# Encoder layer with implicit long filters: the last sums of the spectra, Newton's steps and the direction sums in the filter stage placed on other engines

## The chip, the cores and the metric

The kernel runs on one core of a Trainium2 chip. The metric is the device time of one launch in microseconds. The engines are named as in the profile: PE is TensorE (matmuls), DVE is VectorE, ACT is ScalarE, POOL is GpSimd and SP is SyncE, which only starts transfers here. Each engine works through its own queue in order.

## The reference

The layer normalises its input `x` (1 x 1024 x 1024, f32), projects it, sends the projections through an S5 branch and a Hyena branch, merges both and adds the result to `x`. The change touches the input norm and the stage that makes the Hyena filters. What they compute:

```python
def rmsnorm(x, w):
    y = xf * lax.rsqrt(jnp.mean(xf * xf, axis=-1, keepdims=True) + RMS_EPS)
    return (y * w.astype(jnp.float32)).astype(x.dtype)

def hyena_filters(L, w1, b1, freq, w2, b2, w3, decay):
    ...
    h = jnp.sin(fr * (h @ w2.astype(f32) + b2.astype(f32)))
    h = h @ w3.astype(f32)
    h = h * (jnp.exp(-t * jnp.abs(decay.astype(f32))) + HY_SHIFT)
    h = h.reshape(L, HY_ORDER, HY_DIRS, HY_WIDTH)
    h_fwd, h_bwd = h[:, :, 0], h[:, :, 1]
    k = jnp.concatenate([h_fwd, jnp.zeros_like(h_fwd[:1]), jnp.flip(h_bwd[1:], axis=0)], axis=0)
    k = k * lax.rsqrt(jnp.sum(k * k, axis=0, keepdims=True) + HY_EPS)
    return jnp.fft.rfft(k, axis=0)
```

There are 1024 time steps, two orders and 1024 channels, so 2048 filters of length 2048, and for each its real spectrum.

## The kernel before

The filters are made in eight **units**: two orders `o` times four groups `cq` of 256 channels. The loop in `filters` runs `u` from 0 to 8 and writes three things into each other, a step of each at a time: `filter_time` of unit `u` (eight time blocks of 128 steps, in the order 4, 5, 6, 7, 0, 1, 2, 3), `filter_freq` of unit `u - 1` (twelve steps), and every third step one of `norm_in`, the input norm, which goes on through several units. `filter_norm` of unit `u - 1` is written at the start of a unit with a higher priority. From this text a scheduler makes the order of each engine's queue, and it puts in the waits between engines. A pool's `bufs` says how many buffers a name has; a write into one waits until its last reader is done.

`filter_time`, one block: two matmuls into PSUM give `g`; ScalarE makes the exponential `e`; VectorE multiplies, `e` = (`e` + 0.05) * `g` (L338); ScalarE squares it as `sq` (L342) and GpSimd adds the squares up in `acc` (L357). Then the *direction sums*: the sum and the difference of the two directions (L349, L350), on VectorE for the block numbers in `f_dve0` (first unit) or `f_dve` (the other seven), on GpSimd for the rest. For the first four blocks they go to `so` (one buffer), which is split into a high and a low half, `sh` on ScalarE (L109; VectorE in the first unit) and `sl` on VectorE (L113); for the last four they are `ss` and `sd`, used as they are.

`filter_norm` sums `acc` over the partitions with matmuls into `q`, takes the reciprocal root of two columns (`rsqrt`, L114 to L126), and corrects one row of `ss` of block 0. `norm_in` calls the same `rsqrt` once, with eight columns, and with the result scales the rows `xr` of the input on ScalarE. `rsqrt` starts from an integer guess and makes three Newton steps, each column by itself.

`filter_freq` turns the halves into spectra by matmuls. For `j` = 0 and 1 it makes two odd parts `po` (PSUM, two buffers, L404) and two even parts `pe` (L414); `eo` (ScalarE, L421) is a copy of one even part, `ke` (VectorE, one buffer) the two sums of the even parts. Out of `ke` and each `po` come the sum and the difference, `ko`, which has two buffers (L429, L430), and SP writes `ko` to `kspec` in DRAM (L431). So a unit makes four `ko` tiles of 128 x 1024.

Elsewhere, in `prefetch`, the weights are split by the form that the change brings to `ko`: `wlo` = -`whi` on ScalarE (L511), and a DMA that GpSimd starts adds `wraw` to it in place (L512).

After the last unit come the projections and the S5 branch, whose parameters are loaded through ScalarE's queue.

Of the kernel before, what the change touches and what calls it, by code (L numbers as in the profile page):

```python
# [12 lines left out]
ALU = mybir.AluOpType  # L13
AF = mybir.ActivationFunctionType
# [5 lines left out]
NCH = 256  # L20
# [80 lines left out]
class Trunk:  # L101
# [13 lines left out]
    def rsqrt(self, pool, out, v, n):  # L115

        V = self.nc.vector
        h = pool.tile([128, n], F, name="rsq_h", tag="rsq_h")
        V.tensor_scalar(out=out.bitcast(I32), in0=v.bitcast(I32), scalar1=-0.5, scalar2=float(0x5F3759DF),
                        op0=ALU.mult, op1=ALU.add)  # L120
        V.tensor_scalar(out=v, in0=v, scalar1=-0.5, scalar2=None, op0=ALU.mult)
        for _ in range(3):
            for c in range(n):
                y, z = out[:, c:c + 1], h[:, c:c + 1]
                V.scalar_tensor_tensor(out=z, in0=y, scalar=v[:, c:c + 1], in1=y, op0=ALU.mult, op1=ALU.mult)
                V.scalar_tensor_tensor(out=y, in0=z, scalar=1.5, in1=y, op0=ALU.add, op1=ALU.mult)  # L126

    def reduce_2pi(self, out, x, k):
        nc = self.nc
# [113 lines left out]
    def filters(self, ctx, top):  # L243
        tc = self.tc
        c2 = ExitStack()
        mk = lambda c, n, b, **kw: c.enter_context(tc.tile_pool(name=n, bufs=b, **kw))
        self.f_dve0, self.f_dve = (0, 1, 2, 3, 4, 5), (0, 3)
        sd = [None, mk(ctx, "f_sd1", 1)]
        self.f_w = mk(ctx, "f_work", 2)
        sd[0] = mk(c2, "f_sd0", 1, side="right")  # L250
# [137 lines left out]
    def filter_freq(self, o, cq, sds):  # L388

        nc = self.nc  # L390
# [18 lines left out]
        def even(b0, tiles):  # L409
            pe = pk.tile([128, 2, NCH], F, name="pe", bufs=2)  # L410
            n = len(tiles)
            for part in (1, 0):
                for i, t in enumerate(tiles):
                    nc.tensor.matmul(out=pe[:, part], lhsT=fe[:, b0 + 2 * part + t % 2], rhs=sd[t][part],  # L414
                                     start=part == 1 and i == 0, stop=part == 0 and i == n - 1)
            return pe

        def join(j, po):
            pe = even(8 * j + 4, (2, 3))
            eo = wp.tile([128, 2, NCH], F, name="eo", bufs=1)  # L420
            nc.scalar.copy(out=eo, in_=pe)  # L421
            yield
            pe = even(8 * j, (0, 1))
            ke = wp.tile([128, 2, 2, NCH], F, name="ke", bufs=1)
            nc.vector.tensor_tensor(out=ke[:, 0], in0=pe, in1=eo, op=ALU.add)
            nc.vector.tensor_tensor(out=ke[:, 1], in0=pe, in1=eo, op=ALU.subtract)
            for jj in (j, j + 2):
                ko = wp.tile([128, 4, NCH], F, name="ko")
                nc.vector.tensor_tensor(out=ko[:, 0:2], in0=ke[:, jj // 2], in1=po[jj], op=ALU.add)  # L429
                nc.vector.tensor_tensor(out=ko[:, 2:4], in0=ke[:, jj // 2], in1=po[jj], op=ALU.subtract)  # L430
                nc.sync.dma_start(out=self.kspec[o, cq, jj], in_=ko.rearrange("p a c -> p (a c)"))  # L431

        for j in range(2):
            po = {}
            for jj in (j, j + 2):
                for po[jj] in odd(jj):
                    yield
            yield from join(j, po)
            yield
# [1043 lines left out]
```

## Time and profile before

| | |
|---|---|
| Median of 3 runs | 1446.65 us (1445.04 to 1446.68) |
| The profiled execution, whole | 1447.77 us |
| Its span | 1445.9 us |
| PE busy in the span | 1343.9 us, 93% |
| DVE | 1009.2 us, 70% |
| ACT | 515.7 us, 36% |
| POOL | 379.6 us, 26% |

The shares are means over stages that differ, and the change is made in one of them, the filters, which stand at the start (until about 260 us). So what counts is read there: a *window* is a stretch of the span, given in us from its start, with the busy time of each engine in it; a *wait* is idle time of an engine, put down to the instruction that ended it. "PEclk" is the clock that TensorE was granted, as a share of full speed, which is 2.4 GHz; the lower of the two levels is 1.2 GHz.

### The profile page before, as it was taken

How to read it: one execution, taken by the hardware profiler on the slowest of the kernel's cores; microseconds unless marked ns; L12 is line 12 of the kernel's file. 1: busy time of each engine (PE TensorE's matmuls, PEld its weight loads, DVE VectorE, ACT ScalarE, POOL GpSimd, SP SyncE). 2: the span in 40 equal slices, each digit the busy share in tenths (PEclk: the TensorE clock that was granted, in tenths of full speed). 3: DMA queues.
4: the chain of work that ended last, by engine and by line, in shares of the span. 5: the costliest groups of instructions: out<-in, count | busy, mean ns of one | idle time of the engine just before them, and what ended most of it. 6: DMA issues, size and time to landing. Idle time of an engine off the chain costs nothing.

```text
span 1445.9 us, 19569 instructions
## 1 busy us (share of the span) xinstructions
PE 1343.9 (93%) x7219; PEld 1132.4 (78%) x7219; DVE 1009.2 (70%) x1954; ACT 515.7 (36%) x737; POOL 379.6 (26%) x315
## 2 busy tenths in 40 slices
PE   5888999999999999999999999999999925999998
PEld 3776898888888887878788888888888825978886
DVE  7999997698689877224399994554379984842632
ACT  5576663223233332442322322533322213422322
POOL 3766774000000000232112100343311111432222
PEclk9998999999999999999999999999999967999999
DMA  8211225855784654667956569767788889666332
GB/s 277 90 73 73 89 110 144 199 154 140 201 264 109 139 127 84 167 159 223 315 162 172 178 175 282 195 175 200 254 265 267 268 253 306 184 175 160 119 115 73
DMA packets 188618, 257.23 MB, mean 178 GB/s; under 512 B 23069, under 2 KB 144153, under 8 KB 185788
## 3 DMA queue, kind: packets, MB, share of 16 engines
q1 hardware_dynamic: 149212, 153.69, 34.2%
q0 software_dynamic: 11520, 39.85, 14.6%
q10 hardware_dynamic: 27792, 62.45, 12.1%
q8 instruction: 57, 0.93, 0.3%
q14 instruction: 37, 0.30, 0.1%
HBM read 147.49 MB, written 76.82 MB: 155 GB/s over the span
## 4 chain that ended last, share of the span: by engine, by line
PE 66%; DVE 14%; DMA 8%; issue 2%; ACTq 0%; ACT 0%; SPq 0%; DVEq 0%
PE pps L541 42%; PE iv L634 6%; PE ops L1384 6%; DMA d_y<-x 3%; PE po L404 2%; DMA zc<-c_zc_lo_d 2%; PE fwo L685 2%; PE pe L414 1%; PE fwe L685 1%; DVE st L1216 1%; PE zt L670 1%; DVE st L1214 1%; PE s5ps L1166 1%; DVE e L338 1%; DVE m L719 1%
## 5 line engine op out<-in xcount | busy, mean ns | idle before, releaser
L512 POOL DMA_DIRECT2D wlo<-wraw x76 | 66.8, 879 | 717.8 <-ACT wlo L511 568.3
L541 PE MATMUL pps<-xh,whi 128*128 128x512 f32 x896 | 229.1, 400 | 3.2 <-DVE cv L565 3.2
L541 PE MATMUL pps<-xl,whi 128*128 128x512 f32 x896 | 224.3, 397 | 0.0
L541 PE MATMUL pps<-xh,wlo 128*128 128x512 f32 x896 | 223.9, 396 | 0.0
L541 PEld LDWEIGHTS pps<-xh,whi 128*128 128x128 f32 x896 | 165.9, 189 | 40.1 <-ACT wlo L511 3.6
L541 PEld LDWEIGHTS pps<-xh,wlo 128*128 128x128 f32 x896 | 166.5, 188 | 38.3
L541 PEld LDWEIGHTS pps<-xl,whi 128*128 128x128 f32 x896 | 166.2, 188 | 38.2 <-issue 0.2
L510 ACT CAST whi<-wraw 128x1024 fp32r<-128x1024 f32 (+1 forms) x76 | 74.7, 983 | 310.3 <-PE pps L541 267.9
L404 PE MATMUL po<-sh,fo 128*128 128x256 f32 x512 | 99.8, 289 | 6.9 <-DVE sh L111 5.7
L634 PEld LDWEIGHTS iv<-ic,y 128*128 128x128 f32 x752 | 96.3, 193 | 3.3 <-DVE y L113 0.6
L634 PE MATMUL iv<-ic,y 128*128 128x256 f32 (+1 forms) x752 | 97.7, 285 | 0.0
L113 DVE TENSOR_TENSOR y<-yraw,y 128x512 fp32r<-128x512 f32 x64 | 52.8, 837 | 55.4 <-ACT y L109 54.9
L404 PEld LDWEIGHTS po<-sh,fo 128*128 128x128 f32 x512 | 82.8, 194 | 9.8 <-DVE sh L111 6.7
L511 ACT ACTIVATE wlo<-whi 128x1024 fp32r<-128x1024 f32 (+1 forms) x76 | 74.9, 985 | 20.6 <-PE pps L541 20.4
L357 POOL TENSOR_TENSOR acc<-acc,sq 128x512 f32<-128x512 f32 x56 | 76.4, 1365 | 21.7 <-ACT sq L342 20.0
L404 PE MATMUL po<-sl,fo 128*128 128x256 f32 x256 | 73.4, 287 | 1.0 <-DVE sl L113 1.0
L109 ACT CAST y<-yraw 128x512 fp32r<-128x512 f32 x64 | 39.2, 620 | 76.2 <-PE iv L634 45.9
L563 DVE SCALAR_TENSOR_TENSOR cv<-pps,cw,cv 128x1023 f32<-128x1023 f32 x24 | 30.7, 1280 | 30.4 <-ACT cv L562 30.4
L685 PE MATMUL fwo<-z,zc 128*128 128x256 f32 x384 | 51.7, 288 | 0.0
L404 PEld LDWEIGHTS po<-sl,fo 128*128 128x128 f32 x256 | 49.5, 193 | 2.3 <-DVE sl L113 1.6
L685 PEld LDWEIGHTS fwo<-z,zc 128*128 128x128 f32 x384 | 50.1, 197 | 1.0
L333 PE MATMUL g<-w3h,ha 128*128 128x512 f32 x64 | 32.6, 510 | 18.4 <-DVE e L338 16.6
(437 smaller groups left out, 2662.4 us busy)
## 6 DMA issues: line engine op xcount, KB each, us to landing
wlo<-wraw POOLq DMA_DIRECT2D x64, 512.0 KB, 5.8
wraw<-w_in SPq DMA_DIRECT2D x56, 512.0 KB, 4.7
kspec<-ko SPq DMA_DIRECT2D x32, 512.0 KB, 3.0
kt<-kspec SPq DMA_DIRECT2D x32, 512.0 KB, 5.4
d_y<-x ACTq DMA_DIRECT2D x32, 512.0 KB, 3.9
yraw<-d_y SPq DMA_DIRECT2D x64, 256.0 KB, 4.9
d_m<-cv ACTq DMA_DIRECT2D x16, 512.0 KB, 2.7
d_z<-z ACTq DMA_DIRECT2D x8, 1024.0 KB, 6.1
```

The costliest lines, as they stand in the source:

```text
L109: nc.scalar.copy(out=hi, in_=src)
L113: e.tensor_tensor(out=lo, in0=src, in1=hi, op=ALU.subtract)
L333: nc.tensor.matmul(out=ps, lhsT=ha[:, tsl], rhs=w3h, start=True, stop=False)
L357: nc.gpsimd.tensor_tensor(out=acc, in0=acc, in1=sq, op=ALU.add)
L404: nc.tensor.matmul(out=po[:, part], lhsT=fo[a][:, 12 * (jj % 2) + b], rhs=sd[4 + i][d][:, part], start=n == 0 and part == 0, stop=n == 11 ...
L510: nc.scalar.copy(out=hi, in_=raw)
L511: nc.scalar.activation(out=lo, in_=hi, func=AF.Copy, scale=-1.0)
L512: nc.gpsimd.dma_start(out=lo, in_=raw, accum_op=ALU.add)
L541: nc.tensor.matmul(out=ps[:, hf * 512:hf * 512 + 512], lhsT=w[:, kc], rhs=part(x, kc, hf), start=a == 0 and p == 0 and kc == 0, stop=b == ...
L634: nc.tensor.matmul(out=dst, lhsT=lhsT, rhs=self.ic[b][:, j, cols], start=first, stop=last)
L685: nc.tensor.matmul(out=out, lhsT=zc[a][:, b], rhs=z[:, :, d, zi], start=start and n == 0, stop=stop and n == 3 * len(prods) - 1)
L1384: nc.tensor.matmul(out=pss[cs.start][:, 0:cs.stop - cs.start], lhsT=m[:, kc, ts], rhs=w[kc][:, cs], start=kc == 0 and p == 0, stop=kc == 7 ...
```

## The change

Three things change in the filter stage.

1. `rsqrt` makes each Newton step for all columns at once: h = y * y, h = h * v, y = (h + 1.5) * y. That is nine instructions a call in place of six for each column (12 in `filter_norm`, 48 in `norm_in`).
2. `f_dve` goes from blocks (0, 3) to (0, 2, 4, 6): in each of seven units the direction sums of blocks 2, 4 and 6 are VectorE's, those of 3 go to GpSimd. The first unit stays as it is.
3. `ko` is no longer summed by VectorE. ScalarE writes `po` into its first half and -`po` into its second, and a DMA that GpSimd starts adds `ke`, read twice, to both in place. The write to `kspec` is as it was.

```diff
@@ rsqrt
         for _ in range(3):
-            for c in range(n):
-                y, z = out[:, c:c + 1], h[:, c:c + 1]
-                V.scalar_tensor_tensor(out=z, in0=y, scalar=v[:, c:c + 1], in1=y, op0=ALU.mult, op1=ALU.mult)
-                V.scalar_tensor_tensor(out=y, in0=z, scalar=1.5, in1=y, op0=ALU.add, op1=ALU.mult)
+            V.tensor_tensor(out=h, in0=out, in1=out, op=ALU.mult)
+            V.tensor_tensor(out=h, in0=h, in1=v, op=ALU.mult)
+            V.scalar_tensor_tensor(out=out, in0=h, scalar=1.5, in1=out, op0=ALU.add, op1=ALU.mult)
@@ filters
-        self.f_dve0, self.f_dve = (0, 1, 2, 3, 4, 5), (0, 3)
+        self.f_dve0, self.f_dve = (0, 1, 2, 3, 4, 5), (0, 2, 4, 6)
@@ filter_freq, join
                 ko = wp.tile([128, 4, NCH], F, name="ko")
-                nc.vector.tensor_tensor(out=ko[:, 0:2], in0=ke[:, jj // 2], in1=po[jj], op=ALU.add)
-                nc.vector.tensor_tensor(out=ko[:, 2:4], in0=ke[:, jj // 2], in1=po[jj], op=ALU.subtract)
+                nc.scalar.copy(out=ko[:, 0:2], in_=po[jj])
+                nc.scalar.activation(out=ko[:, 2:4], in_=po[jj], func=AF.Copy, scale=-1.0)
+                nc.gpsimd.dma_start(out=ko.rearrange("p (b a) c -> p b (a c)", b=2), accum_op=ALU.add,
+                                    in_=ke[:, jj // 2].rearrange("p a c -> p (a c)").unsqueeze(1).to_broadcast([128, 2, 2 * NCH]))
                 nc.sync.dma_start(out=self.kspec[o, cq, jj], in_=ko.rearrange("p a c -> p (a c)"))
```

The scheduler moves other instructions with it. On VectorE, at the reciprocal root of the input norm (`rs`, columns of `ssq`), a piece of the queue before was:

```order
L126 SCALAR_TENSOR_TENSOR rs_426<-rsq_h_1012,rs_426 128x1
L125 SCALAR_TENSOR_TENSOR rsq_h_1012<-rs_426,ssq_425 128x1
L126 SCALAR_TENSOR_TENSOR rs_426<-rsq_h_1012,rs_426 128x1
L125 SCALAR_TENSOR_TENSOR rsq_h_1012<-rs_426,ssq_425 128x1
L126 SCALAR_TENSOR_TENSOR rs_426<-rsq_h_1012,rs_426 128x1
L113 TENSOR_TENSOR sl6_1107<-so_1103,sh6_1106 128x512
L125 SCALAR_TENSOR_TENSOR rsq_h_1012<-rs_426,ssq_425 128x1
L126 SCALAR_TENSOR_TENSOR rs_426<-rsq_h_1012,rs_426 128x1 x2
L338 SCALAR_TENSOR_TENSOR e_1184<-e_1184,g_1181 128x512
```

The place that answers to it after the change (line numbers are one less there):

```order
L123 TENSOR_TENSOR rsq_h_1011<-rs_423 128x8
L348 TENSOR_TENSOR ss2_1180<-e_1175 128x256
L349 TENSOR_TENSOR sd2_1181<-e_1175 128x256
L124 TENSOR_TENSOR rsq_h_1011<-rsq_h_1011,ssq_422 128x8
L113 TENSOR_TENSOR sl7_1096<-so_1092,sh7_1095 128x512
L337 SCALAR_TENSOR_TENSOR e_1218<-e_1218,g_1215 128x512
L125 SCALAR_TENSOR_TENSOR rs_423<-rsq_h_1011,rs_423 128x8
L316 TENSOR_TENSOR w3l_1536<-w3_1530,w3h_1535 128x512
L123 TENSOR_TENSOR rsq_h_1011<-rs_423 128x8
L124 TENSOR_TENSOR rsq_h_1011<-rsq_h_1011,ssq_422 128x8
L125 SCALAR_TENSOR_TENSOR rs_423<-rsq_h_1011,rs_423 128x8
```

The one-column pairs are gone; the full-width steps stand apart, with products `e`, a split and a direction sum between them. On ScalarE, in the unit where the rows of the input are scaled (`xr`, four in a row), before:

```order
L336 ACTIVATE e_1863<-dec_1570,negt_89 128x512 [waits Activation_49,Pool_49]
L316 CAST w3h_2222<-w3_2217 128x512 [waits DMAHW1_49,DMAHW0_49,PE_49]
L109 CAST sh7_1786<-so_1783 128x512 [waits DVE_49]
L336 ACTIVATE e_1903<-dec_1570,negt_89 128x512
L342 ACTIVATE sq_1866<-e_1863 128x512 [waits DVE_49,Pool_49]
L468 ACTIVATE xr_555<-xr_555,rs_426 128x512 x4
L336 ACTIVATE e_1985<-dec_1893,negt_89 128x512 [waits Activation_49,Pool_49]
```

After (L428 and L429 are the two new copies of `po`):

```order
L109 CAST sh7_1748<-so_1745 128x512 [waits Pool_49]
L335 ACTIVATE e_1867<-dec_1533,negt_89 128x512
L315 CAST w3h_2187<-w3_2182 128x512 [waits DMAHW7_49,DMAHW1_49,PE_49]
L428 COPY ko_1814<-po_1660 128x512 [waits DMAHW4_49,DMASW2_49]
L429 ACTIVATE ko_1814<-po_1660 128x512
L335 ACTIVATE e_1951<-dec_1857,negt_89 128x512 [waits Activation_49,Pool_49]
L428 COPY ko_1819<-po_1724 128x512 [waits DMAHW5_49,DMASW3_49]
L429 ACTIVATE ko_1819<-po_1724 128x512
L341 ACTIVATE sq_1830<-e_1827 128x512 [waits DVE_49,Pool_49]
L469 ACTIVATE xr_554<-xr_554,rs_423 128x512 x4
```

Two pairs of copies stand between exponentials, squares and casts. The first of each pair waits for two transfers, the write (DMAHW) and the adding DMA (DMASW) of an earlier tile. On GpSimd a piece of the queue of the same unit after the change, where only direction and square sums stood before (L430 is the start of the adding DMA):

```order
L348 TENSOR_TENSOR ss3_1872<-e_1867 128x256 [waits DVE_49]
L349 TENSOR_TENSOR sd3_1873<-e_1867 128x256
L356 TENSOR_TENSOR acc_1629<-acc_1629,sq_1799 128x512 [waits Activation_49,Pool_49]
L430 DMA ko_1814<-ke_1811 128x2x512 [waits DMASW2_49,DMAHW4_49,DVE_49,Activation_49]
L356 TENSOR_TENSOR acc_1629<-acc_1629,sq_1830 128x512 [waits Activation_49,Pool_49]
```

The starts of the adding DMAs stand between the square sums and wait for ScalarE's copies, for VectorE's `ke` and for transfers.

## Rows read from the trace of the kernel before

**Rows 1.** Windows: us; busy us (count) of PE, PEld, DVE, ACT, POOL; PEclk; DMA share; GB/s.

```profile
45.20:69.50 24.30, 20.00 (x119) 16.85 (x118) 24.10 (x48) 14.73 (x25) 19.21 (x19) 1.00 0.29 98
69.50:94.30 24.80, 21.95 (x137) 18.65 (x135) 23.12 (x44) 21.29 (x49) 18.88 (x20) 1.00 0.23 85
94.30:131.40 37.10, 31.28 (x182) 26.37 (x183) 37.03 (x108) 20.22 (x37) 19.06 (x20) 0.86 0.23 86
131.40:157.00 25.60, 22.45 (x144) 19.78 (x144) 25.53 (x49) 18.48 (x32) 19.39 (x20) 1.00 0.24 83
157.00:185.60 28.60, 25.72 (x160) 22.87 (x159) 27.18 (x53) 19.17 (x33) 20.59 (x20) 0.94 0.22 83
185.60:211.60 26.00, 25.61 (x170) 23.11 (x170) 26.00 (x53) 17.66 (x30) 19.23 (x20) 1.00 0.21 83
211.60:237.70 26.10, 24.72 (x166) 22.29 (x165) 24.50 (x49) 12.33 (x21) 19.10 (x20) 1.00 0.26 101
...
281.00:400.00 119.00, 119.00 (x589) 97.42 (x588) 99.55 (x456) 36.39 (x42) 8.70 (x10) 1.00 0.65 174
```

**Rows 2.** Waits of PE, 45.2 to 237.7: total us, count, longest.

```profile
PE g L333 <- DVE e L338: 11.3, 7, 2.4
```

**Rows 3.** VectorE's groups, 45.2 to 237.7: busy us, mean ns | idle before.

```profile
L125 DVE SCALAR_TENSOR_TENSOR rsq_h<-nrm,qs 128x1 f32<-128x1 f32 x42 | 20.6, 523 | 0.2
...
L429 DVE TENSOR_TENSOR ko<-ke,po 128x512 f32<-128x512 f32 x28 | 18.9, 675 | 1.6 <-PE po L404 1.6
L430 DVE TENSOR_TENSOR ko<-ke,po 128x512 f32<-128x512 f32 x27 | 18.2, 674 | 0.0
L350 DVE TENSOR_TENSOR so<-e 128x256 f32<-128x256 f32 x13 | 11.9, 913 | 0.0
...
L126 DVE SCALAR_TENSOR_TENSOR nrm<-rsq_h,nrm 128x1 f32<-128x1 f32 x42 | 9.2, 239 | 0.0
L125 DVE SCALAR_TENSOR_TENSOR rsq_h<-rs,ssq 128x1 f32<-128x1 f32 x24 | 8.2, 355 | 0.0
L349 DVE TENSOR_TENSOR so<-e 128x256 f32<-128x256 f32 x13 | 8.2, 628 | 0.0
...
L126 DVE SCALAR_TENSOR_TENSOR rs<-rsq_h,rs 128x1 f32<-128x1 f32 x24 | 5.4, 236 | 0.0
...
L460 DVE TENSOR_TENSOR ssq<-sums 128x8 f32<-128x8 f32 x1 | 0.2, 155 | 0.0
```

**Rows 4.** ScalarE's L421 and L342: ns min/median/max, first to last start.

```profile
L421 ACT COPY eo<-pe x16: 559/564/587, 48.8 to 251.5; 128x512 f32<-128x512 f32 x16
...
L342 ACT ACTIVATE sq<-e x56: 612/630/637, 20.7 to 230.8; 128x512 f32<-128x512 f32 x56
```

**Rows 5.** GpSimd's groups by line, 0 to 280.

```profile
L357 POOL TENSOR_TENSOR acc<-acc,sq 128x512 f32<-128x512 f32 x56 | 76.4, 1365 | 21.7 <-ACT sq L342 20.0 <-ACT acc L342 1.0
L349 POOL TENSOR_TENSOR ss<-e 128x256 f32<-128x256 f32 x30 | 26.2, 873 | 18.5 <-DVE e L338 10.0 <-DVE e L340 6.3 <-DVE rs L126 2.3
L350 POOL TENSOR_TENSOR sd<-e 128x256 f32<-128x256 f32 x30 | 25.6, 854 | 0.0
```

**Rows 6.** Line L512, the weights' adding DMA: ns on GpSimd, us to landing.

```profile
L512 POOL DMA_DIRECT2D wlo<-wraw x76: 852/869/1202, 244.2 to 1328.5; - x76
...
DMA to landing us min/median/max: 3.3/5.7/21.0
```

**Rows 7.** Line L431, the writes of `ko` to `kspec`.

```profile
DMA to landing us min/median/max: 2.6/3.0/6.9
```

**Rows 8.** Lines L349 and L350, VectorE's sums into `so`: ns min/median/max.

```profile
L349 DVE TENSOR_TENSOR so<-e x18: 403/602/1428, 19.3 to 223.8; 128x256 f32<-128x256 f32 x18
...
L350 DVE TENSOR_TENSOR so<-e x18: 405/946/1521, 19.6 to 224.3; 128x256 f32<-128x256 f32 x18
```

**Rows 9.** Timeline: start us, us, engine, line: `nr` made and used.

```profile
345.32 1.22 DVE L1107 TENSOR_TENSOR nr<-nr,nt 128x1024 f32<-128x1024 f32 x1
...
358.69 1.04 PE L1091 MATMUL s5ps<-ident,nr 128*128 128x128 f32 x8
```

## The prediction

> **What bounds the kernel now.** I read the busy time of each engine unit by unit through the filter stage first, then the waits of TensorE there, then the durations behind them. The profiled execution took 1447.77 us; the median of the three timed runs, 1446.65, is 1.1 below it, so I work out a difference on the profile and take it from the median. The seven windows of [rows 1] run from one `q` sum to the next, each one filter unit: 192.5 us together. VectorE is busy 187.5 of them, TensorE 171.7, GpSimd 135.5, ScalarE 123.9 (the columns added up). So VectorE sets the pace: a span is 1.027 of its busy time. TensorE idles 20.8, and nearly all its waits name VectorE, by far the most the product `e` of L338, 11.3 us in 7 waits [rows 2]. The third window is the odd one: 37.1 us, because Newton's steps for the input norm go through VectorE as 48 one-column instructions. There and in the fifth TensorE was granted 0.86 and 0.94 of full clock. If its busy time is spread evenly, 28% and 12% of it ran at 1.2 GHz instead of 2.4, and half of that, 4.4 + 1.5 = 5.9 us, would come back with a full clock: an estimate. TensorE's own work is then 165.8 us. Behind the filters TensorE is busy 119.00 of 119.00 us (last of [rows 1]), so what the filter stage gains or loses passes on one to one.
>
> **The change part by part**, for these seven windows.
>
> *Last sums.* Out of VectorE go the two 0.675 us sums per `ko` tile, 18.9 + 18.2 = 37.1 us for 28 tiles [rows 3]. Into ScalarE come two instructions per tile, both from PSUM: a copy at 0.564 as `eo` from PSUM, and one with scale -1. No row shows that second form from PSUM; between 0.56 (as `eo`) and 0.64 (a square from SBUF) I take 0.61, nearer the square, since it is an ACTIVATE too [rows 4]. 28 × 1.17 = 32.8, which makes ScalarE 156.7. GpSimd issues 28 adding DMAs at 0.87 [rows 6]: 24.4.
>
> *The adding DMA brings waits.* The weights' DMA is the same form and size, SBUF to SBUF with add: 3.3 us at the least to landing, 5.7 in the middle, 21 at the worst [rows 6]. A `ko` buffer is now held through two copies (1.2), GpSimd's queue (0 to two `acc` sums of 1.365 [rows 5], 2.7), the add (3.3 to 5.7), the write (3.0 [rows 7]) and some 0.3 for the write's own issue, a guess: 7.8 to 12.9 us. There are two buffers and four tiles a unit, so two such turns a unit, 15.6 to 25.8 against units of 24.3 to 28.6. The next unit-half's copy waits for that chain, and behind it on ScalarE stand the exponentials and squares of the following time blocks. I take it as just hidden; the rival below has the price if not. The copies no longer need `ke`, so `po` can come free earlier: I count nothing for that, since waits for `ko` are not among the large ones.
>
> *Newton.* In seven `filter_norm` calls the steps cost 20.6 + 9.2 = 29.8 us, for the input norm 8.2 + 5.4 = 13.6 [rows 3]. Now each call has nine instructions. A 128x8 sum took 0.155 undisturbed, the longer of today's two forms 0.523 on average [rows 3]. I take 0.3, between today's means 0.239 and 0.523, because they meet the same traffic and the next waits on each: 9 × 0.3 = 2.7 a call. Savings: 29.8 - 18.9 = 10.9 (20.0 at 0.155, -3.1 at 0.523) and 13.6 - 2.7 = 10.9 (12.2; 8.9).
>
> *Direction sums.* Block 3 goes to GpSimd; 2, 4 and 6 come to VectorE; net two blocks a unit, 28 instructions. On VectorE they take 0.628 and 0.913 on average [rows 3]: 14 × 1.54 = 21.6, from 14 × (0.403 + 0.405) = 11.3 at the shortest to 14 × (1.428 + 1.521) = 41.3 at the longest [rows 8]. GpSimd loses 14 × (0.873 + 0.854) = 24.2 [rows 5], and with the DMAs stands at 135.7, unchanged.
>
> The spread of the two sums is the point to weigh: 0.403 alone, 1.428 when something holds them, while `ko`, which reads one input from PSUM, stands at 0.675 and 0.674 on average [rows 3]. The Trainium skill, page SBUF — State Buffer, section "Who interferes with whom", states that a VectorE instruction with two SBUF inputs contends with a GpSimd instruction that reads SBUF. It speaks against this change, which swaps instructions that read PSUM for ones that read SBUF twice. By it every new one could pay the long price; by the rows they pay the mean.
>
> *Sum for VectorE:* 187.5 - 37.1 - 10.9 - 10.9 + 21.6 = 150.2 us; with every price at its end, 129 to 185.9. So TensorE (165.8) comes out on top, ScalarE (156.7) close under it.
>
> *By window.* Third: VectorE 37.0 - 10.9 - 1.6 - 5.3 + 3.1 = 22.3, ScalarE 20.2 + 4.7 = 24.9, TensorE 31.3 - 4.4 = 26.9. With some 2 us of friction it takes 29: 8 saved. Second: ScalarE 21.3 + 4.7 = 26.0 in a window of 24.8: 1 lost. The other five idle TensorE 12.1 and lose 1.5 to the clock, 13.6 in all. I let a third come back, 4.5: a choice, because in the fourth ScalarE rises to 23.2, above TensorE's 22.5, and because chains through four engines at 80 to 95% do not pack. Behind the last unit the loads of the S5 parameters stand on ScalarE's queue after the last `ko` copies, which wait for the DMAs: 0 to 2 us, I take 0.5. It is no more because `nr`, the first product made of them, is ready at 346.5 and used at 358.7 [rows 9], 12 us later. Sum: 8 - 1 + 4.5 - 0.5 = 11 us saved, 1446.65 - 11 = 1435.6.
>
> **The rivals.** *Full recovery:* TensorE becomes the bound as cleanly as VectorE is now: 165.8 × 1.027 = 170.3, 22.2 saved, 1424.5. For it: idle named VectorE almost alone. Against: ScalarE's 26.0 in the second window, and the new ring.
>
> *Collisions eat the relief:* every new SBUF-pair instruction pays its long price; VectorE stays at 185.9, times 1.027 is 190.9: 1.6 saved, 1445.0. For it: single rows at 1.4 us today. Against: the means, and as many sums less on GpSimd to collide with. The skill's rule of above is this rival's mechanism.
>
> *The `ko` ring binds (slower):* place: the copy of the next tile at the head of ScalarE's queue, waiting for an add and a write. It decides when a turn exceeds half a mean unit, 27.5 / 2 = 13.75 us. At 14.2 a unit takes 28.4, seven 198.8, 6.3 more than now: 1453. For it: 12.9 us with the middle landing and a full GpSimd queue is near, and the copy may take its buffer before `ke` is there, which lengthens the turn. Against: the filter windows move only 83 to 101 GB/s and keep the DMA engines 21 to 29% busy [rows 1], so the add should land nearer 3.3 than 5.7.
>
> **How the numbers follow.** Forecast as above 56%, full recovery 14%, collisions 13%, ring 17%. Faster by over 0.2% (below 1443.8) takes the first two, 0.70; 0.2% is about what a measurement of this kernel can tell from no change. Within it lie the collisions, 0.13; slower is the ring, 0.17. The range reaches from 1425, which cuts off half of the full recovery, to 1448, past the collisions and the mildest part of the ring: about 0.2 is left out.
>
> **What would show it.** In the changed profile the window with the input norm should be near 29 us with the clock near 1.0; nine Newton instructions a call at about 0.3; VectorE near 150 of the seven windows, ScalarE near 157; TensorE idle half or less of 20.8, its waits naming ScalarE or GpSimd beside VectorE. Full recovery would show TensorE over 95% busy there. The ring shows as ScalarE idle before the `ko` copy, released by a DMA, 2 us or more each. I am wrong if that wait is there in most units, if the sums average over 1.4 us on VectorE, or if a stage behind the filters gives the time back.

## The result: slower by 32 us, and the profile after

The changed kernel takes 1478.95 us (1477.83 to 1482.23), the kernel before 1446.66: a ratio of 1.0228, 95% interval 1.0208 to 1.0248. The prediction was 1435.6 within 1425 to 1448; it is wrong, and in the sign.

In the profiled executions the spans are 1445.9 and 1476.2 us, 30.3 apart. Up to the first `q` sum the changed kernel is 0.6 us ahead. The seven windows from the first `q` to the eighth take 216.5 us in place of 192.4 (+24.1), the stretch from there to the last filter matmul 27.5 in place of 21.9 (+5.6), and all that follows 1187.3 in place of 1186.3. So the loss is made in the filter stage and nothing behind it gives any of it back. The windows of the changed kernel, with their sum, in the columns of [rows 1]:

```profile
44.80:72.10 27.30, 21.73 (x114) 18.65 (x113) 23.65 (x42) 16.30 (x28) 20.72 (x20) 0.94 0.30 66
72.10:100.80 28.70, 22.29 (x140) 20.02 (x138) 21.10 (x38) 22.33 (x51) 19.02 (x18) 0.94 0.73 177
100.80:144.10 43.30, 34.98 (x200) 31.42 (x200) 33.15 (x62) 28.63 (x56) 24.21 (x24) 0.84 0.64 151
144.10:171.60 27.50, 23.52 (x140) 19.84 (x139) 25.58 (x43) 20.13 (x37) 18.79 (x18) 1.00 0.41 105
171.60:199.50 27.90, 24.75 (x153) 22.95 (x152) 21.53 (x42) 21.30 (x38) 21.09 (x20) 0.88 0.66 157
199.50:224.10 24.60, 22.04 (x145) 20.65 (x145) 21.02 (x39) 19.47 (x35) 18.63 (x17) 0.93 0.46 125
224.10:261.30 37.20, 30.88 (x190) 28.25 (x189) 27.96 (x46) 19.66 (x36) 22.33 (x22) 0.91 0.75 178
sum 216.50, PE 180.17 PEld 161.77 DVE 173.99 ACT 147.82 POOL 144.78; mean PE 25.74 PEld 23.11 DVE 24.86 ACT 21.12 POOL 20.68
```

No engine is full any more: VectorE was busy 187.4 of 192.4 us, now 174.0 of 216.5, and TensorE, busy 180.2, idles 36.3 us where it idled 20.8. TensorE is also busy 8.5 us longer for as many matmuls (1082 in place of 1081), since it was granted less than the full clock in six of seven windows (0.84 to 0.94) where before it was two. The longer busy time (8.5) and the longer idle time (15.6) together are the 24.1. They are not spread evenly: the seventh window is 11.1 us longer and the third 6.1, 17.2 of the 24.1.

What the engines wait for in the seven windows, from the waits of ScalarE, VectorE and TensorE (total us, count, longest):

```profile
ACT ko L428 <- DMA kspec<-ko: 24.5, 9, 4.8
...
DVE ke L424 <- DMA ko<-ke: 14.3, 5, 4.0
...
PE g L332 <- DVE e L337: 15.5, 9, 3.2
PE po L403 <- ACT ko L429: 13.4, 5, 5.2
```

Three of these four are new. ScalarE's first copy waits for the write of the tile two back; VectorE's `ke` waits for the adding DMAs, which still read the only `ke` buffer; TensorE's next `po` waits for the copies that stand behind. The old wait for `e` [rows 2] has not shrunk but grown, 11.3 to 15.5 us, though VectorE has less to do. Followed back through these windows, the chain of work that ended last runs over the adding DMA for 14.5% of the time and over the writes of `ko` for 9.8%.

One turn in the fourth unit, from the timelines of ScalarE, VectorE, GpSimd and SP (start us, us, engine, line):

```profile
146.22 0.59 ACT L428 COPY ko<-po 128x512 f32<-128x512 f32 x1 [0.29 <-DMA kspec<-ko]
...
150.24 0.57 ACT L428 COPY ko<-po 128x512 f32<-128x512 f32 x1
...
162.26 0.68 DVE L424 TENSOR_TENSOR ke<-pe,eo 128x512 f32<-128x512 f32 x1
...
163.78 2.42 POOL L430 DMA_DIRECT2D ko<-ke  x2
...
168.88 12.89 SPq L432 DMA_DIRECT2D kspec<-ko  x3
...
171.75 0.69 DVE L424 TENSOR_TENSOR ke<-pe,eo 128x512 f32<-128x512 f32 x1 [1.71 <-DMA ko<-ke]
...
173.69 0.59 ACT L428 COPY ko<-po 128x512 f32<-128x512 f32 x1
```

The two copies take both `ko` buffers at 146.2 and 150.2, but `ke` is made at 162.3. The adds start at 163.8, the first has landed and its write starts at 168.9, and the next copy into that buffer begins at 173.7: one buffer taken for 27.5 us, as long as a mean unit took before (192.4 / 7). That copy shows no wait before it, so this hold, long as it is, cost ScalarE nothing. Of the 28 tiles between the first two and the last two, five had copies that ended 6.7 to 16.5 us before their add was started. Where the add followed within 2 us, copy to write took 6.4 to 9.9 us, and the write another 2.6 to 4.5. Of ScalarE's nine waits for a write, two (7.5 us) stand behind buffers taken for 20.4 and 31.9 us; the other seven (17.0 us) stand behind ordinary turns of 10.7 to 16.0 us, whose adds were started at most 3 us after the copies. One of the first two, in the seventh window, shows how the waits pass on, from the timelines of VectorE, ScalarE and TensorE:

```profile
231.81 0.69 DVE L424 TENSOR_TENSOR ke<-pe,eo 128x512 f32<-128x512 f32 x1 [3.98 <-DMA ko<-ke]
...
233.09 0.59 ACT L428 COPY ko<-po 128x512 f32<-128x512 f32 x1 [3.67 <-DMA kspec<-ko]
...
234.22 0.58 PE L403 MATMUL po<-sh,fo 128*128 128x256 f32 x1 [5.23 <-ACT ko L429]
```

VectorE waits for an add, ScalarE for the write of a buffer taken at 212.7, and TensorE for ScalarE's copies.

The durations behind it are in GpSimd's groups of the seven windows (busy us, mean ns):

```profile
L356 POOL TENSOR_TENSOR acc<-acc,sq 128x512 f32<-128x512 f32 x49 | 74.5, 1520 | 31.7 <-ACT sq L341 22.0 <-ACT acc L341 7.5 <-PE pe L413 1.4
L430 POOL DMA_DIRECT2D ko<-ke x26 | 32.6, 1346 | 10.6 <-ACT ko L429 3.7 <-DVE qs L374 3.2 <-ACT w3h L315 2.1
```

And the time to landing, of the line of the adding DMA and then of the line of the write:

```profile
DMA to landing us min/median/max: 5.0/6.0/8.9
...
DMA to landing us min/median/max: 2.6/3.9/4.5
```

The weights' add, which the prediction took as its price, started in 0.87 us and landed in 3.3 at the least and 5.7 in the middle [rows 6]; this one takes 1.35 in the mean to start and lands in 5.0 at the least and 6.0 in the middle. GpSimd's square sums rose from 1.35 to 1.52 us each.

### The profile page after: what moved, and what is told of

It reads as the page before. It is cut to its first block, busy times and chain, and to the rows that moved or that the text cites. A ratio compares the mean times of both kernels' runs of the same rounds, so it can differ in the third digit from the quotient of the medians.

```text
span 1476.2 us, 19605 instructions
## 1 busy us (share of the span) xinstructions
PE 1357.8 (92%) x7219; PEld 1148.4 (78%) x7219; DVE 994.9 (67%) x1855; ACT 545.9 (37%) x801; POOL 397.2 (27%) x319
## 3 DMA queue, kind: packets, MB, share of 16 engines
q0 software_dynamic: 20224, 56.63, 20.8%
## 4 chain that ended last, share of the span: by engine, by line
PE 63%; DVE 16%; DMA 13%; issue 3%; ACT 3%; POOL 2%; ACTq 1%; SPq 0%; DVEq 0%; POOLq 0%
PE pps L542 41%; PE ops L1385 6%; PE iv L635 4%; DMA ko<-ke 3%; PE fwo L686 2%; DMA kspec<-ko 2%; DMA zc<-c_zc_lo_d 2%; DMA d_y<-x 2%; PE po L403 2%; DVE y L113 1%; PE fwe L686 1%; POOL acc L356 1%; DVE st L1217 1%; PE zt L671 1%; DVE st L1215 1%
## 5 line engine op out<-in xcount | busy, mean ns | idle before, releaser
L542 PEld LDWEIGHTS pps<-xh,whi 128*128 128x128 f32 x896 | 165.8, 189 | 40.2 <-ACT wlo L512 3.6
L403 PE MATMUL po<-sh,fo 128*128 128x256 f32 x512 | 115.7, 317 | 20.5 <-ACT ko L429 15.4
L403 PEld LDWEIGHTS po<-sh,fo 128*128 128x128 f32 x512 | 95.0, 220 | 24.8 <-ACT ko L429 17.2
L113 DVE TENSOR_TENSOR y<-yraw,y 128x512 fp32r<-128x512 f32 x64 | 57.6, 915 | 58.9 <-ACT y L109 58.9
L356 POOL TENSOR_TENSOR acc<-acc,sq 128x512 f32<-128x512 f32 x56 | 84.8, 1515 | 45.4 <-ACT sq L341 35.7
L512 ACT ACTIVATE wlo<-whi 128x1024 fp32r<-128x1024 f32 (+1 forms) x76 | 74.9, 985 | 20.6 <-PE pps L542 20.4
L403 PE MATMUL po<-sl,fo 128*128 128x256 f32 x256 | 80.1, 313 | 1.0 <-DVE sl L113 1.0
L403 PEld LDWEIGHTS po<-sl,fo 128*128 128x128 f32 x256 | 56.7, 221 | 2.6 <-DVE sl L113 1.4
L564 DVE SCALAR_TENSOR_TENSOR cv<-pps,cw,cv 128x1023 f32<-128x1023 f32 x24 | 30.7, 1278 | 32.1 <-ACT cv L563 32.1
```

The costliest lines, as they stand in the source:

```text
L113: e.tensor_tensor(out=lo, in0=src, in1=hi, op=ALU.subtract)
L356: nc.gpsimd.tensor_tensor(out=acc, in0=acc, in1=sq, op=ALU.add)
L403: nc.tensor.matmul(out=po[:, part], lhsT=fo[a][:, 12 * (jj % 2) + b], rhs=sd[4 + i][d][:, part], start=n == 0 and part == 0, stop=n == 11 ...
L512: nc.scalar.activation(out=lo, in_=hi, func=AF.Copy, scale=-1.0)
L542: nc.tensor.matmul(out=ps[:, hf * 512:hf * 512 + 512], lhsT=w[:, kc], rhs=part(x, kc, hf), start=a == 0 and p == 0 and kc == 0, stop=b == ...
```

## The experiments

The two theories I began with were the *ring* (two `ko` buffers, held through copies, `ke`, add and write) and the *sums* (fourteen more direction sums on VectorE, lengthened by GpSimd). All medians, each beside the kernel before on the same chip; "windows" are the seven from the first `q` to the eighth, "tail" the rest up to the last matmul of the filters, in which matmuls of the projections already run. Both are from the one profiled execution, which lay up to 6.0 us off its kernel's median (Newton and direction sums: 1454.2 for 1448.2), so a few us between two rows of these columns tell nothing:

| Kernel | us | to before (95%) | windows | tail |
|---|---|---|---|---|
| before | 1446.7 | | 192.4 | 21.9 |
| after | 1479.0 | 1.0208 to 1.0248 | 216.5 | 27.5 |
| Newton alone | 1452.3 | 1.0035 to 1.0062 | 200.7 | 23.4 |
| direction sums alone | 1452.4 | 1.0024 to 1.0055 | 198.7 | 23.5 |
| last sums alone | 1492.0 | 1.0296 to 1.0346 | 225.1 | 29.2 |
| Newton and direction sums | 1448.2 | 0.9989 to 1.0032 | 196.6 | 23.5 |
| Newton and last sums | 1480.9 | 1.0212 to 1.0272 | 217.2 | 31.6 |
| Newton in the input norm only | 1447.0 | 0.9982 to 1.0011 | 193.3 | 22.8 |
| all direction sums on GpSimd | 1453.7 | 1.0031 to 1.0064 | 196.1 | 22.8 |

### Each part by itself

Newton alone (before, with only `rsqrt` of the change):

```diff
-            for c in range(n):
...
+            V.tensor_tensor(out=h, in0=out, in1=out, op=ALU.mult)
+            V.tensor_tensor(out=h, in0=h, in1=v, op=ALU.mult)
+            V.scalar_tensor_tensor(out=out, in0=h, scalar=1.5, in1=out, op0=ALU.add, op1=ALU.mult)
```

> The kernel before with Newton's steps on all columns at once, and nothing else. Both theories: faster, since VectorE sets the pace there and the new steps take 25.4 + 6.0 us in the changed kernel where the old ones took 29.8 + 13.6: about 12 us of VectorE less, 1435 to 1441 us. If it stays within 3 us of 1446.7, Newton's steps were not on the path.

Measured 1452.3: slower by 6.5, where both theories said faster, and not within 3 us of the kernel before either. Direction sums alone:

```diff
-        self.f_dve0, self.f_dve = (0, 1, 2, 3, 4, 5), (0, 3)
+        self.f_dve0, self.f_dve = (0, 1, 2, 3, 4, 5), (0, 2, 4, 6)
```

> The kernel before with the direction sums of blocks 0, 2, 4 and 6 on VectorE, and nothing else. Theory 'sums' (the direction sums on VectorE, lengthened by GpSimd's work, cost the time): 15 us slower or more, 1462 or above, with single sums of 2 us and more. Theory 'ring' (the two ko buffers, held through copy, ke, adding DMA and write, cost the time): 14 more sums at the old mean of 1.54 us a pair are 21.6 us on a pacing VectorE, less what GpSimd's freed 24 us return: 1450 to 1468, and no sum beyond 1.6 us.

Measured 1452.4, the low end of what the ring theory allowed; no sum took over 1.6 us. Last sums alone:

```diff
-                nc.vector.tensor_tensor(out=ko[:, 0:2], in0=ke[:, jj // 2], in1=po[jj], op=ALU.add)
-                nc.vector.tensor_tensor(out=ko[:, 2:4], in0=ke[:, jj // 2], in1=po[jj], op=ALU.subtract)
+                nc.scalar.copy(out=ko[:, 0:2], in_=po[jj])
+                nc.scalar.activation(out=ko[:, 2:4], in_=po[jj], func=AF.Copy, scale=-1.0)
+                nc.gpsimd.dma_start(out=ko.rearrange("p (b a) c -> p b (a c)", b=2), accum_op=ALU.add,
...
```

> The kernel before with the last sums by ScalarE copies and the adding DMA, and nothing else. Ring: 1470 us or more, with ScalarE waiting 20 us or more for the writes of ko, although VectorE has 37 us less to do. Sums: at most 1446, since VectorE has 37 us less and no new sums.

Measured 1492.0: this one part loses 46 us, with 41.7 us of ScalarE's waits for the writes over the whole stage. Without the direction sums' move:

```diff
-        self.f_dve0, self.f_dve = (0, 1, 2, 3, 4, 5), (0, 2, 4, 6)
+        self.f_dve0, self.f_dve = (0, 1, 2, 3, 4, 5), (0, 3)
```

> The changed kernel with the direction sums left as they were before (blocks 0 and 3 on VectorE). Ring: still 1465 to 1480 us. Sums: 1440 or less, most of the 32 us lost come back.

Measured 1480.9, as slow as the changed kernel and 0.9 above what the ring theory said: the sums theory falls. And the changed kernel with the last sums back on VectorE:

```diff
-                nc.scalar.copy(out=ko[:, 0:2], in_=po[jj])
...
+                nc.vector.tensor_tensor(out=ko[:, 0:2], in0=ke[:, jj // 2], in1=po[jj], op=ALU.add)
+                nc.vector.tensor_tensor(out=ko[:, 2:4], in0=ke[:, jj // 2], in1=po[jj], op=ALU.subtract)
```

> The changed kernel with the last sums left on VectorE as before: Newton's steps and the direction sums alone. Each of the two alone cost 6 to 7 us. If the last sums are the whole loss and the rest adds up: 1452 to 1462. If the two pay together what they don't pay alone (15 us of VectorE's time less against 22 more): 1446 to 1452.

Measured 1448.2, no difference to before that can be told. So the last sums take 30.7 us of the 32, and the other two parts together nothing, though each alone costs 6. Every edit also makes the scheduler write the queues in another order; but no edit of this document that left `ko` as it was moved the time by more than 7 us, so the order by itself is too small a cause for the 30.7.

### Wider rings

Four `ko` buffers; two `ke` buffers; three and two:

```diff
-                ko = wp.tile([128, 4, NCH], F, name="ko")
+                ko = wp.tile([128, 4, NCH], F, name="ko", bufs=4)
```

> The changed kernel with four ko buffers in place of two. Theory 'ko ring' (ScalarE's copy waits for the write of the tile two back, and that is the cost): the 43.9 us that ScalarE waited for kspec fall under 10, and 20 us or more of the 32 come back, 1449 to 1460 us. Theory 'ke ring' (ke has one buffer, held until the adding DMAs have read it, and VectorE waits for it with everything behind): ScalarE's wait goes, but VectorE's waits at ke grow beyond 17 us and the time stays at 1468 or above.

```diff
-            ke = wp.tile([128, 2, 2, NCH], F, name="ke", bufs=1)
+            ke = wp.tile([128, 2, 2, NCH], F, name="ke", bufs=2)
```

> The changed kernel with two ke buffers in place of one, ko as it was. Ko ring: VectorE's 17 us at ke go, but ScalarE's waits for the writes stay above 35 us and the time within 8 us of 1479. Ke ring: 15 us or more come back, 1464 or less.

```diff
+                ko = wp.tile([128, 4, NCH], F, name="ko", bufs=3)
+            ke = wp.tile([128, 2, 2, NCH], F, name="ke", bufs=2)
```

> The changed kernel with three ko buffers and two ke buffers. If the two rings together are the whole loss: 1447 or less. If ScalarE's copies and GpSimd's starts cost time by themselves, or the order of the queues does: 1450 to 1465, with the waits for transfers under 15 us on both engines.

Measured 1469.9, 1468.8 and 1473.6 (ratios to before 1.0161, 1.0163, 1.0192): a third of the loss comes back at most, and both widened together gave no more than either. Neither ring theory as I had put it holds, and the third kernel missed both of its cases. ScalarE's waits for the writes in the windows fell from 24.5 only to 13.7, 15.2 and 17.7 us, and with four `ko` buffers GpSimd's starts waited 17.9 us for `ke`:

```profile
ACT ko L428 <- DMA kspec<-ko: 13.7, 7, 3.5
...
POOL ko L430 <- DVE ke L424: 17.9, 8, 3.3
```

### Taking the add apart

First the changed kernel with the add left out, all else as it is:

```diff
-                nc.gpsimd.dma_start(out=ko.rearrange("p (b a) c -> p b (a c)", b=2), accum_op=ALU.add,
...
```

> The changed kernel without the adding DMA: ke is not added, so the spectra lack their even part; the copies by ScalarE and the writes stay. It takes the add (6.0 us to landing), its start on GpSimd (1.2 us) and the wait for ke out of the ring. Ring theories: a turn falls from 16 to about 6 us, ScalarE's waits for the writes under 5 us, 1435 to 1448 us. If it stays above 1460, the copies on ScalarE or the sums on VectorE are the cost and not the ring.

Measured 1434.6 (ratio 0.9891 to 0.9939). That is the time that the prediction had for the whole change. The sum of the seven windows, in the columns above:

```profile
sum 179.60, PE 164.73 PEld 149.90 DVE 158.69 ACT 147.22 POOL 115.16; mean PE 23.53 PEld 21.41 DVE 22.67 ACT 21.03 POOL 16.45
```

So copies on ScalarE, Newton's steps and direction sums are together not what costs the time: with the add, 44.4 us go. The add has two sides: it lengthens the turn of `ko` and holds `ke`, and it is started by GpSimd. The next two runs have one side each; the third has both, but adds nothing (a plain transfer of the same bytes).

```diff
-                nc.gpsimd.dma_start(out=ko.rearrange("p (b a) c -> p b (a c)", b=2), accum_op=ALU.add,
...
+                nc.sync.dma_start(out=ko.rearrange("p (b a) c -> p b (a c)", b=2),
...
```

> The changed kernel with the adding DMA replaced by a plain transfer of the same bytes that SP starts: ke overwrites ko, so the copies of po are lost from the spectra. The turn of a ko buffer keeps all its steps (copies, ke, transfer, write), GpSimd starts nothing. Theory 'turn' (the length of the turn and the hold on ke cost the time): 1465 or more, ScalarE waiting 25 us or more for the writes. Theory 'GpSimd' (its starts, their waits at the head of its queue and what they do to VectorE cost the time): 1435 to 1450.

```diff
-                nc.gpsimd.dma_start(out=ko.rearrange("p (b a) c -> p b (a c)", b=2), accum_op=ALU.add,
...
-                nc.sync.dma_start(out=self.kspec[o, cq, jj], in_=ko.rearrange("p a c -> p (a c)"))
+                nc.gpsimd.dma_start(out=self.kspec[o, cq, jj], in_=ko.rearrange("p a c -> p (a c)"))
```

> The changed kernel without the adding DMA (ke is not added, the spectra lack their even part), and with the writes of ko started by GpSimd in place of SP: as many GpSimd starts as in the changed kernel, but a short turn that does not need ke. Turn: within 8 us of the 1434.6 of the kernel without the add. GpSimd: 1455 or more.

```diff
-                nc.gpsimd.dma_start(out=ko.rearrange("p (b a) c -> p b (a c)", b=2), accum_op=ALU.add,
...
+                nc.gpsimd.dma_start(out=ko.rearrange("p (b a) c -> p b (a c)", b=2),
...
```

> The changed kernel with the transfer of ke started by GpSimd as there, but plain: it overwrites ko and adds nothing. Theory 'start' (GpSimd's start, waiting for copies and ke at the head of GpSimd's queue, is what the plain transfer from SP did not have): 1470 or more, GpSimd's starts at 1.2 us. Theory 'landing' (an add takes longer to land than a plain transfer, 6.0 against 3.8 us): 1448 to 1460, landing near 3.8 us.

Measured 1448.0, 1443.8 and 1456.8. The first is what the theory 'GpSimd' said, the second lies between its two cases, and the third is what 'landing' said, so neither side is the loss by itself. The steps make a staircase:

| Kernel | us | windows | VectorE busy | GpSimd busy | ScalarE's wait for writes |
|---|---|---|---|---|---|
| no add | 1434.6 | 179.6 | 158.7 | 115.2 | none |
| no add, write started by GpSimd | 1443.8 | 188.1 | 163.0 | 128.4 | none |
| plain transfer started by SP | 1448.0 | 190.3 | 156.2 | 115.2 | 7.8 |
| plain transfer started by GpSimd | 1456.8 | 199.1 | 170.6 | 133.3 | 7.1 |
| the add (after) | 1479.0 | 216.5 | 174.0 | 144.8 | 24.5 |

With the longer turn the time rises by 13.4 us (1434.6 to 1448.0), with the same transfer started on GpSimd by 8.8 more (with the write started there, 9.2), and with adding in place of overwriting by 22.2 more. The first two steps also change the order of the queues, and no run separates the two, so their sizes are not shown to be the turn's and the start's alone. The third step is clear of this: in the traces of the changed kernel and of the plain transfer started by GpSimd, the instructions of every engine stand in the same order up to the end of the filters. These 22.2 us are the add's. With the plain transfer the waits for transfers were

```profile
ACT ko L428 <- DMA kspec<-ko: 7.1, 5, 2.7
...
DVE ke L424 <- DMA ko<-ke: 3.7, 2, 3.4
```

and with the add, as shown above, 24.5 and 14.3.

The second step shows where it is paid: VectorE's busy time rises by 14.4 us for the same instructions. Of this, 8.3 are the direction sums and 3.8 the splits of L113 and L316, which read two operands from SBUF; the products `e`, with one operand in PSUM, stay at 0.68 us each. The Trainium skill, page SBUF — State Buffer, section "Who interferes with whom", states that a VectorE instruction with two SBUF inputs contends with a GpSimd instruction that reads SBUF. The traces agree: the 27 direction sums on VectorE took 1.31 us a pair without the add and 1.73 with it, and one of them held VectorE for 4.65 us while GpSimd ended a start and ran through five sums (timelines of the changed kernel, VectorE and GpSimd):

```profile
250.84 4.65 DVE L348 TENSOR_TENSOR ss<-e 128x256 f32<-128x256 f32 x1
...
248.82 2.43 POOL L430 DMA_DIRECT2D ko<-ke  x2 [0.37 <-DVE ke L424]
250.41 2.17 POOL L356 TENSOR_TENSOR acc<-acc,sq 128x512 f32<-128x512 f32 x1
251.66 1.61 POOL L348 TENSOR_TENSOR ss<-e 128x256 f32<-128x256 f32 x1
252.36 1.61 POOL L349 TENSOR_TENSOR sd<-e 128x256 f32<-128x256 f32 x1
253.05 3.56 POOL L356 TENSOR_TENSOR acc<-acc,sq 128x512 f32<-128x512 f32 x2
```

It is GpSimd's sums that lengthen them, and not a start by itself. Taken one by one from the two timelines of the seven windows, these 54 instructions of VectorE took 0.41 us in the mean where GpSimd did nothing beside them (21), 0.41 where only a start ran (5), 0.86 beside GpSimd's sums (16), and 1.87 beside sums and a start (12).

The third step, 22 us from overwriting to adding, has two candidates: the add lands later, and its start takes longer. The plain transfer's start, in GpSimd's groups of that kernel:

```profile
L430 POOL DMA_DIRECT2D ko<-ke x26 | 18.9, 726 | 7.6 <-issue 2.8 <-ACT ko L429 1.8 <-DVE rsq_h L124 1.5
```

and its landing, from the same line:

```profile
DMA to landing us min/median/max: 3.1/3.4/7.8
```

That is 0.73 and 3.4 us against 1.35 and 6.0. To tell them apart the turn was lengthened without GpSimd, by the plain transfer of SP made twice:

```diff
+                nc.sync.dma_start(out=ko.rearrange("p (b a) c -> p b (a c)", b=2),
...
+                nc.sync.dma_start(out=ko.rearrange("p (b a) c -> p b (a c)", b=2),
...
```

> The kernel with the plain transfer started by SP (1448.0), with that transfer made twice in a row into the same ko, so a turn gets some 4 us longer and GpSimd still starts nothing; ke overwrites the copies. Theory 'landing': the longer turn costs as much as the add's longer landing, 1460 to 1475, ScalarE waiting 35 us or more for the writes. Theory 'start': within 6 us of 1448, since only GpSimd's longer starts and the VectorE sums that they stretch matter.

Measured 1467.6, which is inside what the landing theory said. But the place is another: its windows take 194.1 us, only 3.8 more than with one transfer, and ScalarE's wait for the writes in them is 7.2, not 35. Its tail is 12.5 us longer (33.9 against 21.4), but TensorE is busy in 33.7 of it, because 62 matmuls of the projections run there in place of 20. Behind the tail TensorE then stands idle for 7.4 us in one piece (until 299.3), put down to ScalarE, on whose queue the last copies of `ko` (291.1 and 298.2) stand among the loads of the S5 parameters; with one transfer its longest wait near there is 2.6. In the changed kernel it is the other way round: against the plain transfer started by GpSimd, 17.4 us are lost in the windows and 3.4 in the tail (199.1 and 24.1 there). So the total agreed for another reason. As the queues of this kernel stand in another order than those of the changed one, it does not tell what a longer landing does there.

### Other ways to add

The write first, then the add into DRAM, so that `ko` is free after its write; with one `ke` buffer and with two:

```diff
                 nc.sync.dma_start(out=self.kspec[o, cq, jj], in_=ko.rearrange("p a c -> p (a c)"))
+                nc.gpsimd.dma_start(out=self.kspec[o, cq, jj].rearrange("p (b c) -> p b c", b=2), accum_op=ALU.add,
...
```

> The changed kernel with the add moved behind the write: SP writes the copies of po to kspec, then GpSimd's DMA adds ke to kspec in DRAM. The whole result is computed. A ko buffer is then held through copies and write alone; ke is held until the add. Theory 'turn': ScalarE waits under 10 us for the writes, 1440 to 1455. Theory 'start': GpSimd's starts wait for a write as well, 1465 or more.

> As the kernel that adds in DRAM, with two ke buffers, so that VectorE does not wait for the add either. Turn: 1436 to 1448, at best as fast as the kernel without the add. Start: within 8 us of the kernel with one ke buffer.

Measured 1481.8 and 1464.5: the first in the range of 'start', the second in neither of its cases. With one buffer ScalarE's wait is gone (6.4 us once in the whole stage), and VectorE waits in its place, 40.5 us at `ke` for the add, which now takes 7.9 us to land:

```profile
DVE ke L424 <- DMA kspec<-ke: 40.5, 7, 9.2
```

The second `ke` buffer takes that away and gives back 17 us, but 19 over the kernel before remain. Then half of the tiles summed by VectorE, half by the add:

```diff
+                if jj == j:
+                    nc.vector.tensor_tensor(out=ko[:, 0:2], in0=ke[:, jj // 2], in1=po[jj], op=ALU.add)
+                    nc.vector.tensor_tensor(out=ko[:, 2:4], in0=ke[:, jj // 2], in1=po[jj], op=ALU.subtract)
+                else:
...
```

> The changed kernel with every first tile of a pair summed by VectorE as before, and only the second by copies and the adding DMA. VectorE gets 18.5 us back, the ring half its transfers. If the loss goes with the number of adds: about half, 1455 to 1465. If one add a half unit is hidden: 1440 to 1450.

Measured 1465.6, 0.6 above the range for half the loss, a ratio of 1.0117 to 1.0153: 20 of 32 us, so the loss goes roughly with the number of adds.

### The premise that VectorE's load sets the pace

Newton alone had been slower though it took work off VectorE, so two more runs went there:

```diff
-        self.f_dve0, self.f_dve = (0, 1, 2, 3, 4, 5), (0, 3)
+        self.f_dve0, self.f_dve = (0, 1, 2, 3, 4, 5), ()
```

> The kernel before with all direction sums of the last seven units on GpSimd: the opposite of the change's second part. VectorE's load falls by 14 pairs at 1.54, 21.6 us, GpSimd's rises by 24 to about 160 of 192. If VectorE's load paces the filters: 1425 to 1440. If the order of the queues and chains between engines pace them: 1443 or more.

```diff
         for _ in range(3):
+            if n > 2:
...
+                continue
             for c in range(n):
```

> The kernel before with Newton's steps on all columns at once in the input norm alone (48 instructions become 9), the eight filter norms as before. If the 7 us that Newton alone lost come from the filter norms' order: 1436 to 1443, some 10 us of VectorE less. If they come from the input norm's place among the units: 1448 to 1456.

Measured 1453.7 and 1447.0: slower, and the same, the second in neither of its cases. The sum of the windows with Newton alone:

```profile
sum 200.70, PE 177.10 PEld 154.64 DVE 180.76 ACT 124.80 POOL 131.89; mean PE 25.30 PEld 22.09 DVE 25.82 ACT 17.83 POOL 18.84
```

and with all direction sums on GpSimd:

```profile
sum 196.10, PE 168.82 PEld 148.41 DVE 170.16 ACT 122.72 POOL 150.14; mean PE 24.12 PEld 21.20 DVE 24.31 ACT 17.53 POOL 21.45
```

Before, the same windows took 192.4 with VectorE busy 187.4 and TensorE 171.6. VectorE loses 6.6 and 17.2 us of work, and the windows get longer by 8.3 and 3.7. In the first, TensorE is busy 5.5 us longer for as many matmuls, with less than the full clock in five windows where before it was two, and idle 2.8 longer. That the new orders of the queues are worse by themselves fits, but no run here keeps the order and changes the work alone, so it is argued and not shown. What is shown is that 6 to 17 us less on VectorE (6 in the input norm's case) buy nothing in this stage.

## Why the prediction was wrong, point by point

**The step that failed** is "I take it as just hidden": the waits that the adding DMA brings had no price in the sum. They are not hidden: in the seven windows ScalarE waits 24.5 us for the writes, VectorE 14.3 for the adds, and TensorE 13.4 for ScalarE's copies. The kernel without the add is 44.4 us faster than the changed one, and the add costs 22.2 against a plain transfer with every queue in the same order.

**Without the add** the sum came close: predicted 1435.6, measured 1434.6; the windows 192.5 - 11.5 = 181.0 and 179.6, TensorE 165.8 predicted and 164.7 measured, VectorE 150.2 and 158.7, ScalarE 156.7 and 147.2. In part this is luck. The forecast had 24.4 us of starts on GpSimd, which this kernel has not; with the writes started there, it took 1443.8. The third window took 31.7 us where 29 was forecast, and the five other than the second and third, 126.1 in the forecast, took 121.9. And both engines were mis-sized, since the records of neighbours on one engine overlap, so that the durations of a group add up to more than the busy time that it brings or takes away: in the changed kernel the 53 copies of ScalarE add up to 31.6 us (those of one tile start 0.49 us apart and last 0.59 and 0.60), and its busy time rose by 23.9.

**The ring rival** had the right place (the first copy of a tile at the head of ScalarE's queue) and a price a fourth of the loss in the windows, 6.3 us where they lost 24.1. Its terms: the add's landing was taken from [rows 6], 3.3 to 5.7, as the same form, and measured 6.0 (5.0 at the least); the start 0.87, and measured 1.35. I leaned to the low end because the DMA engines were only 21 to 29% busy; the plain transfer bears that out (3.1 to 3.4 us), the add does not. That copies may take their buffer long before `ke` is there stood in a half sentence without a price; in the trace it held `ko` for up to 27.5 us, but only 7.5 of the 24.5 us of waits stand behind such holds. What the rival had wrong is its condition, a turn of more than half a mean unit, 13.75 us: seven waits stand behind turns of 10.7 to 16.0, six of them below 13.75, because the copies come in close pairs and not evenly over a unit. And only one ring was counted: `ke`, with its single buffer, had been free after VectorE's own sums and is now held until the adds have read it, which is VectorE's 14.3 us.

**GpSimd** stood at "135.7, unchanged" and was taken as harmless because its busy time was the same. But its queue stood idle for 10.6 us before starts in the seven windows, with square sums behind them, and VectorE's sums took longest where a start and GpSimd's sums ran beside them (1.87 us, and 0.86 beside sums alone). A transfer started by GpSimd in place of SP went with 8.8 and 9.2 us more, the new order of the queues included. The collisions rival had the mechanism and tied it to the moved direction sums; these, with Newton's steps, cost nothing.

**Newton's steps** were sized at 0.3 us each, 2.7 a call; in the changed kernel the three instructions took 11.6 + 7.5 + 6.3 = 25.4 us for seven filter norms, 3.6 a call, and 6.0 for the input norm. Against 29.8 and 13.6 before [rows 3] the saving was 12.0 us and not 21.8 (16.7 without the add). The third window went to 43.3 and not 29.

**The direction sums** were sized at 1.54 us a pair; they took 1.31 without the add, 1.73 with it.

**"VectorE sets the pace"** was read from its busy share, 187.5 of 192.5. The three edits that lighten VectorE a little gained nothing, so a share of 97% named the engine that is fullest, not the one whose time passes through one to one. Taking 37 us of `ko` sums away and leaving out the add did pay (1448.2 to 1434.6, 13.6), about a third of it.

**What held:** the filter stage's loss passes on one to one (+1.0 us in 1187 behind it), and the wait that was to show the ring, ScalarE idle before the `ko` copy and released by a DMA, is the one that the trace shows.

**What stays open:** through which property the add takes its 22.2 us. With the queues in the same order, the waits for transfers grew by 17.4 us on ScalarE and by 10.6 on VectorE, which speaks for the longer landing (3.4 to 6.0 us); but the start is longer too (0.73 to 1.35), the square sums are slower (1.37 to 1.52), and no run has one of them without the others. Nor is it shown how much of the 13.4 and 8.8 us of the other two steps is the turn and the start, and how much the new order of the queues.

## What to carry to other kernels

A sum that is moved from an engine into a transfer is priced by the turn of every buffer that it touches, the one that it reads (`ke`) as well as the one that it writes: from the first write into the buffer, through waiting for the other operand, to the landing of the last transfer. Before such a move, run the kernel with the transfer left out, and with a plain one in its place: the first says what the rest of the change is worth (here 12 us), the second, if the same engine starts it, what the add itself costs (here 22). Compare the order of the queues of the two kernels first: only where it is the same is the difference the edit's alone. And a busy share near one doesn't make an engine's time pass through; here 6 to 17 us less of it bought nothing.

## What the runs showed of the hardware

An adding DMA of 512 KB within SBUF, reading its source twice, took 5.0 us at the least and 6.0 in the middle from the beginning of its start to landing; the plain one of the same shape from the same queue took 3.1 and 3.4, and from SP 3.1 and 3.8. The Trainium skill, page DMA: Bandwidth & Descriptors, section "Anatomy of one DMA — SWDGE (gpsimd) path", gives 2.0 us plus the bytes over 436 GB/s for a transfer that GpSimd starts, by which 512 KB would take 3.2, an estimate; the plain transfer agrees with it, the add does not. GpSimd was held 0.57 us by the start of a write to DRAM, 0.73 by that of the plain transfer, and 1.35 by that of the add. A sum of two SBUF operands of 128 x 256 took VectorE 0.41 us with GpSimd idle or only starting a transfer, 0.86 in the mean beside GpSimd's sums, and 1.87 beside sums and a start. TensorE's granted clock was 1.00 in six of the seven windows without the add, and 0.84 to 0.94 in six of seven with it; there it stood at the lower level, 1.2 GHz, in seven stretches, 37.5 us together, each of which began within or shortly behind a pause of TensorE of 2.3 to 5.2 us.
